# Gate matrix of an expert layer: float32 one-hot products replaced by three bfloat16 products per token

## The chip, the cores and the metric

The kernel runs on one core of a Trainium2 chip. The core has TensorE (PE, matrix products, with its weight loads shown apart as PEld), VectorE (DVE), ScalarE (ACT), GpSimd (POOL) and SyncE (SP, which here issues the DMAs). The metric is the device time of one execution in microseconds (us).

## What is computed

A two-layer encoder over 512 tokens of width 1024. Layer 0 mixes tokens by neighbourhood attention, layer 1 by a short gated convolution; behind each stands a PEER channel mixer over 128 x 128 = 16384 experts of one neuron each:

```
q = (xc @ w_query).reshape(c, 8, 2, 128)              # 8 heads, two halves
sc = einsum('chpd,hpnd->chpn', q, keys32)
sv, si = top_k(sc, 16)                                # per half
cand = sv[:, :, 0, :, None] + sv[:, :, 1, None, :]
best, pos = top_k(cand, 16)                           # 16 experts per head
eidx = take_along_axis(cidx, pos)                     # i * 128 + j
g = softmax(best)
a = einsum('cd,chkd->chk', xc, w_up[eidx])
act = gelu(a) * g
y = einsum('chk,chkd->cd', act, w_down[eidx])
```

So each token has 128 chosen experts (i, j) with a gate g each.

## The kernel before

**Two ways for the tokens.** Of the four chunks of 128 tokens, the last gets its experts' rows one by one (indirect DMAs, L475). The other three (384 tokens, `TD`) are computed densely: for every block `b` of 128 experts, `dense_up` multiplies all 384 tokens with the block's up weights and takes the gelu, and `dense_down` multiplies that with the gates and then with the down weights. For this each token needs its gates as a full matrix of 128 x 128, which is zero but for its 128 experts.

**The gate matrix.** That matrix is itself a product on PE: per token, a one-hot of the 128 chosen `i` (tile `ob`, from `iT`) and a one-hot of the 128 chosen `j`, scaled with the gates (tile `oa`, from `jT` and `gT`). `retrieval` goes over the 384 tokens in groups of four (96 groups per layer, 192 in all): DVE makes `ob` (L448) and `oa` (L452 for two of the tokens, scaled by ACT at L458; L460 for the two others), PE makes four products of 128 x 128 x 128 in float32 (L462, recorded as two passes each), ACT moves the result from PSUM to `stage` (L463). After 32 tokens `stage` is written to the buffer `gd` in DRAM (L466). The expert phase reads it back by blocks of experts, tile `gt` (L516); a read of `gt` takes from all twelve writes of the layer, so the first one comes after the last write.

**Products in two halves.** The dense products are float32 split in a high and a low part (`split`, L105 on ACT and L106 on DVE): three products with 384 columns for `ps_up` (L127), three with 512 columns for `acc` (L541). An up block has 24 products on PE.

**Order.** While DVE selects the experts and makes the one-hots, PE is given the up products of the first 52 blocks (`NPRE`); their results go to DRAM (`ad`). The generator `retrieval` tells the loop at L552 by its `yield` how much DVE and PE time its pieces take, and the loop puts up products between them. The order in the program is then set anew for each engine by the framework's scheduler as the kernel is built; on the chip each engine takes its instructions in that fixed order, and waits for semaphores. Up to six results of up blocks beyond the 52 are held on chip (`AHEAD`), so that a few more up blocks may be done before the expert phase begins. That phase's first step is `w`, the product of an up result with `gt` (L525), then its split `w_h`, `w_l`, then the first `acc`.

Of the kernel before, what the change touches and what calls it, by code (L numbers as in the profile page):

```python
# [12 lines left out]
F32 = mybir.dt.float32  # L13
F32R = mybir.dt.float32r
BF16 = mybir.dt.bfloat16
I32 = mybir.dt.int32
U32 = mybir.dt.uint32
AF = mybir.ActivationFunctionType
ALU = mybir.AluOpType
# [4 lines left out]
P = 128  # L24
# [16 lines left out]
NK = 128  # L41
# [8 lines left out]
TD = ND * P  # L50
NPRE = 52
PRE_RATE = 1.4
OB = 12
ACTN = 2
RING = 4
RAW = 3
LAST = 2
# [7 lines left out]
def encoder(ctx: ExitStack, tc: tile.TileContext, x, g_mix, g_ffn, g_ffn_row, g_fin_row, bias,  # L65
            w_qkv, w_o, w_in, w_conv, w_out, w_query, keys_t, up_t, up, down, out):
    nc = tc.nc
    const = ctx.enter_context(tc.tile_pool(name="const", bufs=1))
# [9 lines left out]
    iota = const.tile([P, P], F32, name="iota")  # L78
    nc.gpsimd.iota(iota, pattern=[[1, P]], base=0, channel_multiplier=0,
                   allow_small_or_imprecise_dtypes=True)  # L80
    thr = const.tile([P, TOPK], BF16, name="thr")
    ranks = const.tile([P, TOPK], BF16, name="ranks")
    for r in range(TOPK):
# [10 lines left out]
    def ps_acc(name):  # L94
        return ps_a.tile([P, 512], F32, name=name, tag="acc")
# [18 lines left out]
    def up_block(src, xh, xl, n):  # L114
        for ps in up_pieces(src, xh, xl, n):
            pass
        return ps
# [263 lines left out]
    def peer(l):  # L381
        xh, xl = norm_t(gf[:, l], f"f{l}")
        with ExitStack() as st:
            pp = st.enter_context(tc.tile_pool(name="peer", bufs=1))
            head = ExitStack()
            p2 = head.enter_context(tc.tile_pool(name="retrieval", bufs=2))
# [8 lines left out]
            for hp in range(2 * PH):  # L395
                kt = p2.tile([P, NK], F32, name="kt")
                nc.sync.dma_start(kt, keys_t[l, hp])
                ps = up_block(w_query[l, hp], xh, xl, S)
                qT = p2.tile([P, S], F32, name="qpT")
                nc.scalar.activation(qT, ps, AF.Copy)  # L400
                ps = ps_acc("ps_k")
                for c in range(NCH):
                    nc.tensor.matmul(ps[:, c * NK:(c + 1) * NK], qT[:, c * P:(c + 1) * P], kt, start=True, stop=True)  # L403
                hd, p = divmod(hp, 2)
# [4 lines left out]
            cand = p2.tile([P, PH, NCAND], F32, name="cand", bufs=1)  # L409
            nc.gpsimd.memset(cand, LOWEST)  # L410
            gT = p2.tile([P, TD], F32, name="gT", bufs=1)
            iT = p2.tile([P, TD], F32, name="iT", bufs=1)
            jT = p2.tile([P, TD], F32, name="jT", bufs=1)
            eid = pp.tile([P, P], F32, name="eid")
            eidx = pp.tile([P, P], I32, name="eidx")
            g3 = pp.tile([P, P], F32, name="g3")
# [1 line left out]
            pr = p2  # L418

            def retrieval():  # L420

                for c in (3, 0, 1, 2):
                    it = select(sv[:, c], si[:, c], pr, cand)
                    while True:
                        try:
                            yield next(it), 0.0
                        except StopIteration as e:
                            gg, ii, jj = e.value
                            break
                    if c == c3:  # L430
                        nc.vector.scalar_tensor_tensor(eid, ii, float(NK), jj, op0=ALU.mult, op1=ALU.add)
                        if l:
                            nc.vector.tensor_scalar(eid, eid, float(l * NK * NK), None, op0=ALU.add)
                        nc.vector.tensor_copy(eidx, eid)
                        nc.vector.tensor_copy(g3, gg)
                    else:
                        ps = ps_acc("ps_g")
                        for n, t in enumerate((gg, ii, jj)):
                            nc.tensor.transpose(ps[:, n * P:(n + 1) * P], t, ident)
                        for n, t in enumerate((gT, iT, jT)):  # L440
                            nc.vector.tensor_copy(t[:, c * P:(c + 1) * P], ps[:, n * P:(n + 1) * P])
                for t0 in range(0, TD, GT):
                    stage = pr.tile([P, NK, GT], F32, name="stage", tag="big")
                    for q in range(GT // 4):
                        ps = ps_acc("ps_gb")
                        t = t0 + 4 * q
                        b4 = pr.tile([P, 4, NK], F32, name="ob", bufs=OB // 4)
                        nc.vector.tensor_tensor(b4, iota[:, None, :].to_broadcast([P, 4, NK]),  # L448
                                                iT[:, t:t + 4, None].to_broadcast([P, 4, NK]), op=ALU.is_equal)
                        a4 = pr.tile([P, 4, NK], F32, name="oa", bufs=OB // 4)  # L450
                        if ACTN:
                            nc.vector.tensor_tensor(a4[:, :ACTN], iota[:, None, :].to_broadcast([P, ACTN, NK]),  # L452
                                                    jT[:, t:t + ACTN, None].to_broadcast([P, ACTN, NK]),
                                                    op=ALU.is_equal)
                        for n in range(4):
                            a, t = a4[:, n], t0 + 4 * q + n
                            if n < ACTN:
                                nc.scalar.activation(a, a, AF.Copy, scale=gT[:, t:t + 1])  # L458
                            else:
                                nc.vector.tensor_scalar(a, iota, jT[:, t:t + 1], gT[:, t:t + 1],  # L460
                                                        op0=ALU.is_equal, op1=ALU.mult)
                            nc.tensor.matmul(ps[:, n * NK:(n + 1) * NK], a, b4[:, n], start=True, stop=True)  # L462
                        nc.scalar.activation(stage[:, :, 4 * q:4 * q + 4].rearrange("p i t -> p t i"),  # L463
                                             ps.rearrange("p (t i) -> p t i", t=4), AF.Copy)
                        yield 1.35, 0.9
                    nc.sync.dma_start(gd[t0 // GT], stage)  # L466

# [84 lines left out]
            for d, p in retrieval():  # L552
                dve += d
                pe += p
                while pe < dve * PRE_RATE and next(pre, 0) is None:
                    pe += 0.49
# [3 lines left out]
            p2 = st.enter_context(tc.tile_pool(name="experts", bufs=2))  # L560
# [111 lines left out]
    for l in range(DEPTH):  # L672
        if l % 2 == 0:
            attention(l)
        else:
            short_conv(l)
        peer(l)
# [76 lines left out]
```

## Time and profile before

| | |
|---|---|
| median of 3 runs | 2993.33 us (2993.03 to 2993.86) |
| profiled execution, its own time | 2994.69 us |
| span of its instructions | 2992.9 us |
| PE busy | 2952.2 us (99%) |
| DVE busy | 2345.6 us (78%) |
| ACT busy | 1360.9 us (45%) |
| granted TensorE clock, mean | 0.996 |

The durations are those of the profiled execution; its time is 1.4 us above the median and 1.8 us above its span. Busy time of PE counts modelled ends, so products that follow each other overlap in the records: how fast they go is read from their starts.

### The profile page before, as it was taken

How to read it: one execution, taken by the hardware profiler on the slowest of the kernel's cores; microseconds unless marked ns; L12 is line 12 of the kernel's file. 1: busy time of each engine (PE TensorE's matmuls, PEld its weight loads, DVE VectorE, ACT ScalarE, POOL GpSimd, SP SyncE). 2: the span in 40 equal slices, each digit the busy share in tenths (PEclk: the TensorE clock that was granted, in tenths of full speed). 3: DMA queues.
4: the chain of work that ended last, by engine and by line, in shares of the span. 5: the costliest groups of instructions: out<-in, count | busy, mean ns of one | idle time of the engine just before them, and what ended most of it. 6: DMA issues, size and time to landing. Idle time of an engine off the chain costs nothing.

```text
span 2992.9 us, 43780 instructions
## 1 busy us (share of the span) xinstructions
PE 2952.2 (99%) x15570; PEld 2636.1 (88%) x15570; DVE 2345.6 (78%) x5115; ACT 1360.9 (45%) x2237; POOL 663.4 (22%) x571
## 2 busy tenths in 40 slices
PE   8999999999999999999999999999999999999998
PEld 6777899999888888888878789999988888888886
DVE  5445999886888888878864489998788888888786
ACT  5453257994333333333332323699733333333333
POOL 0000000002343444343400000000043434444341
PEclk9999999999999999999999999999999999999999
DMA  5323355659999999999933324556799999999995
GB/s 187 106 81 96 95 161 168 240 214 328 335 337 346 335 343 329 337 343 324 320 113 93 117 87 129 166 216 217 261 352 348 334 347 332 338 330 346 325 329 190
DMA packets 297979, 747.93 MB, mean 250 GB/s; under 512 B 23456, under 2 KB 139168, under 8 KB 294688
## 3 DMA queue, kind: packets, MB, share of 16 engines
q1 hardware_dynamic: 224032, 476.67, 46.5%
q0 software_dynamic: 73728, 268.47, 24.7%
q8 instruction: 122, 2.00, 0.3%
q14 instruction: 97, 0.79, 0.1%
HBM read 672.17 MB, written 72.88 MB: 249 GB/s over the span
## 4 chain that ended last, share of the span: by engine, by line
PE 91%; DVE 4%; issue 2%; DMA 2%; ACT 1%; POOL 0%; DVEq 0%; POOLq 0%; SPq 0%
PE ps_up L127 45%; PE acc L541 33%; PE ps_gb L462 6%; PE ps_o L191 3%; DVE wu_l L106 1%; PE ps_k L403 1%; PE ps_s L260 1%; PE ps_o L300 1%; DMA row<-in_up,eidx 1%; PE ps_pt L286 1%; DMA gd<-stage 0%; PE ps_t L175 0%; POOL row L475 0%; DVE tk L600 0%; ACT sq L150 0%
## 5 line engine op out<-in xcount | busy, mean ns | idle before, releaser
L127 PE MATMUL ps_up<-xhf,wu_l 128*128 128x384 f32 (+1 forms) x2304 | 798.4, 347 | 1.1 <-DVE wu_l L106 1.0
L127 PE MATMUL ps_up<-xhf,wu_h 128*128 128x384 f32 (+1 forms) x2304 | 794.3, 345 | 2.3 <-ACT ab L504 2.0
L127 PE MATMUL ps_up<-xlf,wu_h 128*128 128x384 f32 (+1 forms) x2304 | 792.4, 344 | 0.0
L105 ACT ACTIVATE wu_h<-wu_raw 128x1024 fp32r<-128x1024 f32 x336 | 355.4, 1058 | 688.8 <-PE ps_up L127 413.2
L475 POOL DMA_INDIRECT row<-in_up,eidx x256 | 325.1, 1270 | 1277.9 <-DMA wu_raw<-in_up_t 848.5
L541 PE MATMUL acc<-wd_h,w_l 128*128 128x512 f32 x1536 | 601.4, 392 | 0.1
L541 PE MATMUL acc<-wd_l,w_h 128*128 128x512 f32 x1536 | 601.2, 391 | 0.0
L105 ACT ACTIVATE wd_h<-wd_raw 128x1024 fp32r<-128x1024 f32 x256 | 271.5, 1061 | 699.2 <-issue 591.0
L106 DVE TENSOR_TENSOR wu_l<-wu_raw,wu_h 128x1024 fp32r<-128x1024 f32 x336 | 411.1, 1224 | 191.2 <-ACT wu_h L105 190.1
L541 PE MATMUL acc<-wd_h,w_h 128*128 128x512 f32 x1536 | 513.0, 391 | 0.9 <-ACT w_h L105 0.9
L106 DVE TENSOR_TENSOR wd_l<-wd_raw,wd_h 128x1024 fp32r<-128x1024 f32 x256 | 313.6, 1225 | 231.3 <-ACT wd_h L105 230.7
L127 PEld LDWEIGHTS ps_up<-xhf,wu_h 128*128 128x128 f32 x2304 | 433.3, 188 | 20.9 <-ACT ab L504 3.4
L127 PEld LDWEIGHTS ps_up<-xlf,wu_h 128*128 128x128 f32 x2304 | 433.1, 188 | 17.3
L127 PEld LDWEIGHTS ps_up<-xhf,wu_l 128*128 128x128 f32 x2304 | 433.1, 188 | 16.8 <-DVE wu_l L106 3.8
L475 POOL DMA_INDIRECT row<-in_down,eidx x256 | 332.4, 1298 | 510.4 <-DVE sq L482 471.8
L541 PEld LDWEIGHTS acc<-wd_h,w_l 128*128 128x128 f32 x1536 | 288.2, 188 | 59.5 <-DVE w_l L106 1.2
L491 DVE SCALAR_TENSOR_TENSOR accg<-row,ag,accg 128x1024 f32<-128x1024 f32 x256 | 327.9, 1281 | 15.8 <-DMA row<-in_down,eidx 15.1
L541 PEld LDWEIGHTS acc<-wd_l,w_h 128*128 128x128 f32 x1536 | 288.3, 188 | 59.0
L541 PEld LDWEIGHTS acc<-wd_h,w_h 128*128 128x128 f32 x1536 | 287.0, 188 | 55.3 <-ACT w_h L105 2.3
L482 DVE SCALAR_TENSOR_TENSOR sq<-row,hn 128x1024 bf16<-128x1024 f32 x256 | 312.5, 1221 | 6.2 <-DMA row<-in_up,eidx 5.0
L462 PE MATMUL ps_gb<-ob,oa 128*128 128x128 f32 x1536 | 209.4, 274 | 0.0
L463 ACT ACTIVATE stage<-ps_gb 128x512 f32<-128x512 f32 x192 | 204.5, 1114 | 2.0 <-PE ps_gb L462 1.4
(162 smaller groups left out, 3262.6 us busy)
## 6 DMA issues: line engine op xcount, KB each, us to landing
wd_raw<-in_down SPq DMA_DIRECT2D x256, 512.0 KB, 6.0
wu_raw<-in_up_t SPq DMA_DIRECT2D x256, 512.0 KB, 5.1
gd<-stage SPq DMA_DIRECT2D x24, 2048.0 KB, 7.2
gt<-gd SPq DMA_DIRECT2D x64, 768.0 KB, 9.6
ad<-ab SPq DMA_DIRECT2D x104, 192.0 KB, 2.4
at<-ad SPq DMA_DIRECT2D x52, 384.0 KB, 8.1
wu_raw<-in_w_query SPq DMA_DIRECT2D x32, 512.0 KB, 3.5
wu_raw<-in_w_qkv SPq DMA_DIRECT2D x24, 512.0 KB, 3.7
```

The costliest lines, as they stand in the source:

```text
L105: nc.scalar.activation(hi, raw, AF.Copy)
L106: nc.vector.tensor_tensor(lo, raw, hi.bitcast(F32), op=ALU.subtract)
L127: nc.tensor.matmul(ps[:, :n], a[:, c], b[:, kc, :n], start=k == 0, stop=k == 3 * KC - 1)
L191: nc.tensor.matmul(ps[c], a[:, m, c * P:(c + 1) * P], b, start=m == 0 and i == 0, stop=m == KC - 1 and i == 2)
L260: nc.tensor.matmul(ps[hh][:, a * 256:(a + 1) * 256], t["q"][hs, j * P:(j + 1) * P], kk[hs, :, BAND0[j]:BAND0[j] + BAND], start=True, stop= ...
L286: nc.tensor.transpose(pt[:, i * P:(i + 1) * P], sc[:, a, half * P:(half + 1) * P], ident)
L462: nc.tensor.matmul(ps[:, n * NK:(n + 1) * NK], a, b4[:, n], start=True, stop=True)
L463: nc.scalar.activation(stage[:, :, 4 * q:4 * q + 4].rearrange("p i t -> p t i"), ps.rearrange("p (t i) -> p t i", t=4), AF.Copy)
L475: nc.gpsimd.indirect_dma_start(out=t, out_offset=None, in_=table, in_offset=bass.IndirectOffsetOnAxis(ap=eidx[:, k:k + 1], axis=0))
L482: nc.vector.scalar_tensor_tensor(o, t, 1.0, hn, op0=ALU.mult, op1=ALU.mult, accum_out=ag[:, k:k + 1])
L491: nc.vector.scalar_tensor_tensor(accg, t, ag[:, k:k + 1], accg, op0=ALU.mult, op1=ALU.add)
L541: nc.tensor.matmul(acc[c, half], aa[:, cs], ww[:, hs], start=new and i == 0, stop=n == NK - 1 and ww is held[-1][-1])
```

## The change

The gates are split exactly into three bfloat16 parts (tile `gp`): the first is the gate rounded to bfloat16, the next the rounded rest, the third the rest of that. The indices go to bfloat16 (`ijT`, exact up to 127). Both one-hots of four tokens come from one DVE operation (`hot`, 2 x 128 x 4 elements, token innermost), and a second one multiplies the `j` half with the three parts (`cut`, 3 x 128 x 4). PE then makes three bfloat16 products per token into one PSUM sum, 12 per group, with operands that lie four elements apart. The eviction reads PSUM in another order and writes runs of four to `stage`. ACT no longer scales one-hots.

```diff
@@ -78,6 +77,8 @@
+    iota4 = const.tile([P, NK, 4], BF16, name="iota4")
+    nc.vector.tensor_copy(iota4, iota[:, :, None].to_broadcast([P, NK, 4]))
@@ -409,8 +410,8 @@
             gT = p2.tile([P, TD], F32, name="gT", bufs=1)
-            iT = p2.tile([P, TD], F32, name="iT", bufs=1)
-            jT = p2.tile([P, TD], F32, name="jT", bufs=1)
+            ijT = p2.tile([P, 2, TD], BF16, name="ijT", bufs=1)
+            gp = p2.tile([P, 3, TD], BF16, name="gp", bufs=1)
@@ -437,31 +438,32 @@
-                        for n, t in enumerate((gT, iT, jT)):
-                            nc.vector.tensor_copy(t[:, c * P:(c + 1) * P], ps[:, n * P:(n + 1) * P])
+                        cs = slice(c * P, (c + 1) * P)
+                        for n, t in enumerate((gT[:, cs], ijT[:, 0, cs], ijT[:, 1, cs])):
+                            nc.vector.tensor_copy(t, ps[:, n * P:(n + 1) * P])
+
+                        for n in range(3):
+                            nc.vector.tensor_copy(gp[:, n, cs], gT[:, cs])
+                            if n < 2:
+                                nc.vector.tensor_tensor(gT[:, cs], gT[:, cs], gp[:, n, cs], op=ALU.subtract)
...
-                        b4 = pr.tile([P, 4, NK], F32, name="ob", bufs=OB // 4)
-                        nc.vector.tensor_tensor(b4, iota[:, None, :].to_broadcast([P, 4, NK]),
-                                                iT[:, t:t + 4, None].to_broadcast([P, 4, NK]), op=ALU.is_equal)
-                        a4 = pr.tile([P, 4, NK], F32, name="oa", bufs=OB // 4)
-                        if ACTN:
-                            nc.vector.tensor_tensor(a4[:, :ACTN], iota[:, None, :].to_broadcast([P, ACTN, NK]),
-                                                    jT[:, t:t + ACTN, None].to_broadcast([P, ACTN, NK]),
-                                                    op=ALU.is_equal)
+                        hot = pr.tile([P, 2, NK, 4], BF16, name="hot", bufs=OB // 4)
+                        nc.vector.tensor_tensor(hot, iota4[:, None].to_broadcast([P, 2, NK, 4]),
+                                                ijT[:, :, None, t:t + 4].to_broadcast([P, 2, NK, 4]),
+                                                op=ALU.is_equal)
+                        cut = pr.tile([P, 3, NK, 4], BF16, name="cut", bufs=OB // 4)
+                        nc.vector.tensor_tensor(cut, hot[:, 1:2].to_broadcast([P, 3, NK, 4]),
+                                                gp[:, :, None, t:t + 4].to_broadcast([P, 3, NK, 4]), op=ALU.mult)
                         for n in range(4):
-                            a, t = a4[:, n], t0 + 4 * q + n
-                            if n < ACTN:
-                                nc.scalar.activation(a, a, AF.Copy, scale=gT[:, t:t + 1])
-                            else:
-                                nc.vector.tensor_scalar(a, iota, jT[:, t:t + 1], gT[:, t:t + 1],
-                                                        op0=ALU.is_equal, op1=ALU.mult)
-                            nc.tensor.matmul(ps[:, n * NK:(n + 1) * NK], a, b4[:, n], start=True, stop=True)
-                        nc.scalar.activation(stage[:, :, 4 * q:4 * q + 4].rearrange("p i t -> p t i"),
-                                             ps.rearrange("p (t i) -> p t i", t=4), AF.Copy)
+                            for i in range(3):
+                                nc.tensor.matmul(ps[:, n * NK:(n + 1) * NK], cut[:, i, :, n], hot[:, 0, :, n],
+                                                 start=i == 0, stop=i == 2)
+                        nc.scalar.activation(stage[:, :, 4 * q:4 * q + 4],
+                                             ps.rearrange("p (t i) -> p i t", t=4), AF.Copy)
                         yield 1.35, 0.9
```

The scheduler gives the instructions another order, though the `yield` values are the same. On PE, before, the last gate groups of layer 0 stand among single up products (`xhf`, `xlf` are the two halves of the activations, `wu_h`, `wu_l` those of the weights; a row `ps_gb` x4 is one group):

```order
L127 MATMUL ps_up<-xhf_2381,wu_h 128x384
L127 MATMUL ps_up<-xlf_2382,wu_h 128x384
L462 MATMUL ps_gb<-ob,oa 128x128 x4
L127 MATMUL ps_up<-xhf_2381,wu_l 128x384
L127 MATMUL ps_up<-xhf_2381,wu_h 128x384
L127 MATMUL ps_up<-xlf_2382,wu_h 128x384
L127 MATMUL ps_up<-xhf_2381,wu_l 128x384
L462 MATMUL ps_gb<-ob,oa 128x128 x4
L127 MATMUL ps_up<-xhf_2381,wu_h 128x384
L127 MATMUL ps_up<-xlf_2382,wu_h 128x384
```

The second of these two groups is the layer's last. From there 95 up products follow on PE, in both layers, up to the first products of the expert phase, which stand so:

```order
L127 MATMUL ps_up<-xhf_2381,wu_l 128x384
L127 MATMUL ps_up<-xhf_2381,wu_h 128x384
L127 MATMUL ps_up<-xlf_2382,wu_h 128x384
L541 MATMUL acc_7311<-wd_h,w_h 128x512
L541 MATMUL acc_7315<-wd_h,w_h 128x512
```

At the same place of PE, with the change, the last rows of layer 0's gate products and the first of the expert phase are (LDWEIGHTS is the load of one part of `cut`, which is an instruction of its own for bfloat16):

```order
L463 LDWEIGHTS cut
L463 MATMUL ps_gb<-hot,cut 128x128
L463 LDWEIGHTS cut
L463 MATMUL ps_gb<-hot,cut 128x128
L543 MATMUL acc_7712<-wd_h,w_h 128x512
L543 MATMUL acc_7716<-wd_h,w_h 128x512
```

No up product is left between the two in layer 0, and 9 are in layer 1. Within the stretch from the first gate product to the last, 840 and 831 up products stand in the two layers in place of 675, and 577 in place of 601 between the last key scores and the first gate product; most of the stretch now goes in turns of 36 gate products (three groups) and 25 up products.

On DVE, the one-hots of those three groups stand together, with one low half of an up block's weights (`wu_l`) in each turn:

```order
L107 TENSOR_TENSOR wu_l<-wu_raw,wu_h 128x1024
L455 TENSOR_TENSOR hot<-iota_82,ijT 128x1024 x2
L459 TENSOR_TENSOR cut<-hot,gp 128x1536
L455 TENSOR_TENSOR hot<-iota_82,ijT 128x1024
L459 TENSOR_TENSOR cut<-hot,gp 128x1536 x2
L107 TENSOR_TENSOR wu_l<-wu_raw,wu_h 128x1024
```

Before, a group had `ob`, one `oa` of 256 elements and two `oa` of 128 there, and the groups stood one by one.

## Rows read from the trace of the kernel before

**Rows 1.** The page: busy time by engine, and the granted clock in 40 slices.

```profile
PE 2952.2 (99%) x15570; PEld 2636.1 (88%) x15570; DVE 2345.6 (78%) x5115; ACT 1360.9 (45%) x2237; POOL 663.4 (22%) x571
...
PEclk9999999999999999999999999999999999999999
```

**Rows 2.** Windows: us, busy of PE, PEld, DVE, ACT, POOL, clock; last `ps_gb` alone.

```profile
450.00:486.00 36.00, 35.00 (x202) 34.33 (x201) 35.22 (x131) 23.05 (x29) 0.00 (x0) 1.00 0.49 156
500.00:650.00 150.00, 150.00 (x1069) 150.00 (x1069) 133.37 (x316) 139.31 (x258) 0.00 (x0) 1.00 0.63 227
...
500.00:650.00 150.00, 78.15 (x575) 76.60 (x576) 75.68 (x71) 1.00 0.63 227
```

**Rows 3.** Timeline of PE, dense products: start us, length, instruction.

```profile
698.27 0.33 PE L127 MATMUL ps_up<-xhf,wu_h 128*128 128x384 f32 x1
...
706.24 0.34 PE L127 MATMUL ps_up<-xlf,wu_h 128*128 128x384 f32 x1
...
712.08 0.39 PE L541 MATMUL acc<-wd_h,w_h 128*128 128x512 f32 x1
...
715.48 0.39 PE L541 MATMUL acc<-wd_h,w_h 128*128 128x512 f32 x1
```

**Rows 4.** Groups of gate instructions: count, busy us, mean ns, idle before.

```profile
L462 PE MATMUL ps_gb<-ob,oa 128*128 128x128 f32 x1536 | 209.4, 274 | 0.0
...
L463 ACT ACTIVATE stage<-ps_gb 128x512 f32<-128x512 f32 x192 | 204.5, 1114 | 2.0 <-PE ps_gb L462 1.4
L448 DVE TENSOR_TENSOR ob<-iota,iT 128x512 f32<-128x512 f32 x192 | 132.1, 690 | 23.8 <-PE ps_gb L462 21.3
L458 ACT ACTIVATE oa<-oa,gT 128x128 f32<-128x128 f32 x384 | 130.5, 390 | 28.0 <-DVE oa L452 27.9
L460 DVE TENSOR_SCALAR oa<-iota,jT,gT 128x128 f32<-128x128 f32 x384 | 115.7, 345 | 0.0
...
L452 DVE TENSOR_TENSOR oa<-iota,jT 128x256 f32<-128x256 f32 x192 | 80.9, 421 | 0.0
```

**Rows 5.** Timeline of PE around one gate group.

```profile
599.77 1.05 PE L462 MATMUL ps_gb<-ob,oa 128*128 128x128 f32 x8
600.58 0.42 PE L127 MATMUL ps_up<-xhf,wu_l 128*128 128x384 f32 x1
600.84 0.34 PE L127 MATMUL ps_up<-xhf,wu_h 128*128 128x384 f32 x1
```

**Rows 6.** Timeline of the hand-off in layer 0, all engines.

```profile
689.05 1.05 PE L462 MATMUL ps_gb<-ob,oa 128*128 128x128 f32 x8
...
690.14 1.11 ACT L463 ACTIVATE stage<-ps_gb 128x512 f32<-128x512 f32 x1
691.27 0.33 SPq L466 DMA_DIRECT2D gd<-stage  x1
...
698.65 1.76 SPq L516 DMA_DIRECT2D gt<-gd  x2
...
705.57 0.56 DVE L525 TENSOR_TENSOR w<-ab,gt 128x384 f32<-128x384 f32 x1 [5.48 <-DMA gt<-gd]
...
706.79 1.63 PE L541 MATMUL acc<-wd_h,w_h 128*128 128x512 f32 x6 [0.21 <-ACT w_h L105]
```

**Rows 7.** PE's timeline ahead of layer 1's experts; two windows, clock and GB/s.

```profile
1718.69 0.66 PE L175 MATMUL ps_t<-ident,hs 128*128 128x128 f32 x2 [5.39 <-issue]
...
1717.00:1724.00 7.00, 5.31 (x25) 5.23 (x26) 4.99 (x28) 3.55 (x10) 0.00 (x0) 0.52 0.27 75
691.00:698.00 7.00, 7.00 (x42) 7.00 (x42) 1.23 (x1) 1.92 (x4) 0.00 (x0) 1.00 0.96 378
```

**Rows 8.** Groups of DVE instructions that resemble the new ones.

```profile
L106 DVE TENSOR_TENSOR wu_l<-wu_raw,wu_h 128x1024 fp32r<-128x1024 f32 x336 | 411.1, 1224 | 191.2 <-ACT wu_h L105 190.1
...
L643 DVE TENSOR_TENSOR msk<-msk,ds 128x2048 bf16<-128x2048 bf16 x16 | 19.8, 1240 | 0.0
...
L648 DVE TENSOR_TENSOR msk<-msk 128x1024 bf16<-128x1024 bf16 x16 | 11.3, 706 | 0.0
```

More of the change, by code (lines that the diff above doesn't have):

```diff
@@ L53 @@
 OB = 12
-ACTN = 2
 RING = 4
```

## The prediction

> **What bounds the kernel now.** I read the busy shares first. TensorE (PE) is busy through the whole span and its clock is full in every slice [rows 1]; the other engines have room. Then the stretch that the change touches, the gate products, by windows: from 500 to 650 us PE is busy 150.0 of 150.0 us, ScalarE (ACT) 139.3, VectorE (DVE) 133.4 [rows 2]. A busy PE may hide short waits, since its ends are modelled, so I checked the start-to-start steps in the timeline. Dense products of 384 columns start from 698.27 to 706.24 us in 46 steps, 173.3 ns each; those of 512 columns from 712.08 to 715.48 in 15 steps, 226.7 ns each [rows 3]. The difference is 53.4 ns for 128 columns, and above its columns each product costs 173.3 - 160.2 = 13 ns. PE keeps these steps through the stretch, so its own work sets the pace there, and what it saves there is saved in the end, unless a wait appears.
>
> Last I looked at the way out of the stretch in the timeline: the last `stage` goes to DRAM and comes back as `gt` before the expert phase can begin [rows 6].
>
> **The gate products.** They are 192 groups of 4 tokens, 8 passes each [rows 4]. One group stands at 599.77 us, the next product at 600.58, and the one after that 0.26 us later in place of 0.173 [rows 5]: 0.81 + 0.087 = 0.897 us per group, 112 ns per pass. That is two times 53.4 ns plus 5 ns: a float32 pass streams its 128 columns at half rate. 192 x 0.897 = 172.2 us.
>
> After, a group is 12 pairs of weight load and product with 128 bfloat16 columns. No row shows one. If the columns stream at full rate and the load hides, a pair costs 53.4 ns plus what a product costs above its columns: 5 ns by the short passes of now, 13 by the long dense ones, so 59 or 67 ns. I take 63, as the pair is short like the first and streams at full rate like the second. 12 x 63 = 0.756 us, 145.2 in all: **-27.0 us** (-36.3 at 59, -17.8 at 67).
>
> **The hand-off to the expert phase.** In the order of before, 95 up products stand on PE between the last gate product and the first `acc`; in the order of the change none in the first layer, 9 in the second. What lies between takes its time on other queues [rows 6]: the last gate group starts at 689.05 us and frees PE at 689.95; `stage` is evicted from 690.14, its write to `gd` is issued at 691.27, the read `gt` at 698.65 when the write has landed, `w` starts at 705.57, and after it and its high half the first `acc` at 706.79. That is 16.8 us, and the 95 products (95 x 0.173 = 16.5) cover all but some 0.4 us of it. The second layer's hand-off has the same instructions and 95 products too, so I take it as equal. The up products that stood there are not gone, they stand earlier, where PE was full already; PE's total stays and the chain becomes idle time: 16.8 + (16.8 - 9 x 0.173) - 2 x 0.4 = **+31 us**. The bounds: with fewer weight loads beside it, the write can be shorter. From 691 to 698 us the queues moved 378 GB/s, the 2 MB of `gd` being only part [rows 7]; 2.1 MB at that rate take 5.5 us in place of 7.3, and as much may be gained on `gt`: 13 us per layer, +23.5. A slower eviction adds a microsecond per layer, +33.
>
> **The clock after the gap.** After PE stood idle for 5.4 us up to 1718.7, the granted clock was 0.52 over 1717 to 1724, near its lower level of 1.2 GHz [rows 7]. A gap of 15 us should do it too. Half speed for 3.4 to 7 us costs 1.7 to 3.5 us per layer; I take **+3.4 us** for both, 0 and +7 as ends.
>
> **DVE's way to the first gate product.** Per chunk of tokens the change adds three casts and two subtractions of 128x128. The nearest row, an `oa` of that size, takes 345 ns [rows 4], so they take up to 1.7 us per chunk and 5.2 per layer of three chunks. From 450 to 486 us DVE is busy 35.2 of 36.0 us, and PE, 35.0 busy, already waits 1.0 us [rows 2]; with the change 577 up products cover PE there in place of 601, 24 x 0.173 = 4.2 us less. The cost is nothing if the order keeps PE fed, and 9 us per layer if nothing does. I take 3, since most of the casts stand between other work of DVE after the first gate product has its operands: **+6 us**.
>
> **What costs nothing.** The one-hots on DVE: now 690 + 421 + 2 x 345 = 1801 ns per group [rows 4]. `hot` has 1024 elements in bfloat16 and `cut` 1536; bfloat16 two-input operations take 706 ns for 1024 and 1240 for 2048, also with an operand that repeats [rows 8], so 706 + 971 = 1677 ns. DVE has no more to do than now, and PE's stream covers it. ACT loses two scalings of 390 ns per group [rows 4]; nobody waited for them for long, so this gains nothing. The eviction reads PSUM with a hop for each element and writes runs of 4, where it now reads a run and writes with hops (1114 ns); I take the same 1.1 us, which ACT's freed time covers. The `iota4` copy at the start lies beside the first loads.
>
> **Sum.** -27.0 + 31 + 3.4 + 6 = +13.4 us on the profiled execution's own 2994.7, so 3008.1; the median of the runs is 1.4 lower: **3007 us**, 0.4% slower. 0.2%, 6 us, is about what a measurement of this kernel can tell from no change. With these terms the change pays only if a pair p takes less than 57 ns (192 x (0.897 - 12p) = 40.4). The case's own range is 2997 to 3025: the pair's ends, and up to half of what hand-off, clock and DVE's way may add.
>
> **The rivals.**
> *The hand-off shrinks (faster).* If it takes 13 us per layer, DVE's way to the first product costs 2 us in all, and pairs take 59 ns: -36.3 + 23.5 + 3.4 + 2 = -7.4, so **2986**. With that hand-off it isn't faster once a pair takes 62 ns or more. For it: the queues moved more than the write alone. Against: both transfers have a landing time that fewer neighbours don't remove, and 13 us is the end of my bounds.
> *No change.* Pairs at 59 ns with all else as in the sum: +4, so **2997**.
> *The weight load doesn't hide.* A 128-column bfloat16 product gives the load of the next 128 columns only 53 ns, where the passes of now give it 107 [rows 5]. If it shows in part, a pair lies between 67 and the 112 of now; the middle, 90, gives 1.08 us per group, +35 + 40 = +75, so **3069** (3120 at 112). For it: no product here is that short. Against: the passes of now show only 5 ns above their columns. The Trainium skill ("TensorE: Matmul & The Clock Gate", section "Back-to-back issue gap") puts a steady stream of load and product at 128 columns at about 81 ns; no run here shows that yet, and it would give 972 ns per group and some 3047 us.
> *DVE runs the new operands at one element per cycle*, as the float32 split does (1024 in 1224 ns [rows 8]): 1224 + 1760 per group is 1.2 us more than now, 115 us per layer where DVE has 23 to spare: about **3190**. Against it: `msk` repeats an operand and keeps the fast rate.
> *The eviction becomes the limit.* ACT has 139.3 us for 71 groups [rows 2], 1.96 each; without the scalings 1.18, the eviction's 1.11 among them. PE's group then takes 2.11 - 0.897 + 0.756 = 1.97, so ACT binds once the eviction takes 1.9 us. At 2.0 us some 20 us come on top: **3027**.
>
> **How the numbers follow.** The sum 0.40, no change 0.20, faster 0.15, the weight load 0.15, DVE 0.05, eviction 0.05. So faster 0.15, same 0.20, slower 0.65. Below 2984 and above 3060 lies about 0.2: the far end of the faster case, the upper half of the weight loads, and DVE.
>
> **What would show it.** Right: steps of 59 to 67 ns from one gate product to the next; PE idle once per layer, 13 to 17 us, right behind the last gate group, released by `w_h`, with a lower granted clock behind it; `hot` near 700 and `cut` near 970 ns; ACT's share in the stretch down by a third. Wrong: no idle time there, since the order would then not be what sets it; steps over 80 ns; PE waiting for `cut` all through the stretch.

## The result, and the profile after

| | before | changed |
|---|---|---|
| median of 4 runs each | 2993.3 us (2993.0 to 2993.9) | 3133.5 us (3131.9 to 3135.6) |
| profiled execution, its own time | 2994.7 us | 3135.6 us |
| ratio | | 1.0468, 95% interval 1.0455 to 1.0481 |

The changed kernel is slower by 140 us, where 14 were forecast; the case's own range ended at 3025 us, 32 above the kernel before, and 3060 us was the upper mark of the chances. The page of the changed kernel, busy time by engine:

```profile
PE 3062.8 (98%) x16338; PEld 2729.3 (87%) x16338; DVE 2360.5 (75%) x4762; ACT 1179.8 (38%) x1853; POOL 659.3 (21%) x571
```

TensorE is still the busy engine, and its mean granted clock is 0.990 (0.996 before): a difference of 0.006 is at most some 19 us of the 3134, so no loss of clock explains 140. The groups of the gate stage, over the whole span (count, busy us, mean ns, idle before), which answer to [rows 4]:

```profile
L463 PE MATMUL ps_gb<-hot,cut 128*128 128x128 bf16 x2304 | 286.6, 297 | 0.0
L459 DVE TENSOR_TENSOR cut<-hot,gp 128x1536 bf16<-128x1536 bf16 x192 | 178.0, 953 | 0.1
L455 DVE TENSOR_TENSOR hot<-iota,ijT 128x1024 bf16<-128x1024 bf16 x192 | 132.2, 690 | 138.1 <-PE ps_gb L463 137.7
L465 ACT ACTIVATE stage<-ps_gb 128x512 f32<-128x512 f32 x192 | 115.0, 599 | 253.0 <-PE ps_gb L463 253.0
L446 DVE CAST gp<-gT 128x128 bf16<-128x128 f32 x18 | 4.0, 224 | 0.0
L448 DVE TENSOR_TENSOR gT<-gT,gp 128x128 f32<-128x128 f32 x12 | 3.4, 286 | 0.0
```

VectorE's two operations take 690 and 953 ns, and `hot` now waits 137.7 us in all for `ps_gb`: VectorE stands behind TensorE, not the other way round. ScalarE waits for it too, and its eviction takes 599 ns in place of 1114. TensorE's timeline around one turn of three gate groups, to be held against [rows 5]:

```profile
605.20 4.41 PE L463 MATMUL ps_gb<-hot,cut 128*128 128x128 bf16 x36
609.35 0.42 PE L128 MATMUL ps_up<-xlf,wu_h 128*128 128x384 f32 x1
609.62 0.34 PE L128 MATMUL ps_up<-xhf,wu_l 128*128 128x384 f32 x1
```

The mean length of a record, 297 ns, says little, since the records overlap. The starts do: from 605.20 to 609.35 there are 36 products, and the first up product behind them takes 0.27 us to the next start in place of 0.173. That makes (4.15 + 0.097) / 36 = **118 ns per pair** of load and product, 1.415 us per group. Before, a group took 0.897. 192 x 0.518 is 99 us.

The hand-off in layer 0, all engines, to be held against [rows 6]:

```profile
767.90 1.58 PE L463 MATMUL ps_gb<-hot,cut 128*128 128x128 bf16 x12
...
770.14 0.33 SPq L468 DMA_DIRECT2D gd<-stage  x1
...
777.40 1.16 SPq L518 DMA_DIRECT2D gt<-gd  x2
...
782.72 0.56 DVE L527 TENSOR_TENSOR w<-ab,gt 128x384 f32<-128x384 f32 x1 [12.48 <-DMA gt<-gd]
783.36 0.52 ACT L106 ACTIVATE w_h<-w 128x384 fp32r<-128x384 f32 x1 [13.25 <-DVE w L527]
...
783.94 1.65 PE L543 MATMUL acc<-wd_h,w_h 128*128 128x512 f32 x3 [14.46 <-ACT w_h L106]
...
2307.15 2.93 PE L543 MATMUL acc<-wd_h,w_h 128*128 128x512 f32 x6 [12.75 <-ACT w_h L106]
```

The chain of before stands there without its cover: TensorE is idle for 14.5 us, released by `w_h`, and for 12.8 us in layer 1 (last row). Windows of the changed kernel (us, busy of PE, PEld, DVE, ACT, POOL, granted clock, DMA share, GB/s):

```profile
500.00:650.00 150.00, 150.00 (x1060) 145.71 (x1059) 102.54 (x132) 55.98 (x88) 0.00 (x0) 1.00 0.47 176
784.00:787.50 3.50, 3.50 (x9) 2.92 (x10) 2.73 (x5) 1.17 (x3) 0.00 (x0) 0.50 1.05 389
787.50:791.00 3.50, 3.50 (x15) 3.41 (x14) 1.89 (x4) 0.00 (x0) 1.19 (x2) 0.68 1.03 408
450.00:486.00 36.00, 32.36 (x183) 30.94 (x182) 34.96 (x130) 20.74 (x24) 0.00 (x0) 1.00 0.42 141
```

Behind the gap the clock stands at 0.50, which is 1.2 GHz, and then at 0.68: 3.5 x 0.5 + 3.5 x 0.32 = 2.9 us are lost in this layer; in layer 1 it is 0.50 from 2307 to 2311 us, another 2. Ahead of the gate stage TensorE is busy for 32.4 of 36 us in layer 0, where it was 35.0 [rows 2], and for 32.8 in layer 1 (1975 to 2011 us; 35.0 in the same stretch before): 2.6 and 2.2 us more of idle time. In layer 1 the clock also falls to 0.57 there from 1998 to 2002 us, another 1.7 us. So 99 (products) + 27.3 - 0.8 (hand-off) + 5 + 1.7 (clock) + 4.8 (ahead of the first gate product) = 137 of the 140.9 us between the profiled executions; 4 are not assigned. Open was why a pair takes 118 ns.

### The profile page after: what moved, and what is told of

It reads as the page before. It is cut to its first block, busy times and chain, and to the rows that moved or that the text cites. A ratio compares the mean times of both kernels' runs of the same rounds, so it can differ in the third digit from the quotient of the medians.

```text
span 3133.8 us, 44260 instructions
## 1 busy us (share of the span) xinstructions
PE 3062.8 (98%) x16338; PEld 2729.3 (87%) x16338; DVE 2360.5 (75%) x4762; ACT 1179.8 (38%) x1853; POOL 659.3 (21%) x571
## 4 chain that ended last, share of the span: by engine, by line
PE 46%; DVE 3%; DMA 1%; issue 0%; ACT 0%; DVEq 0%; ACTq 0%; SPq 0%
PE ps_up L128 22%; PE acc L543 17%; PE ps_gb L463 4%; PE ps_o L192 1%; DVE wu_l L107 1%; PE ps_k L404 0%; PE ps_t L176 0%; DMA row<-in_down,eidx 0%; DMA gd<-stage 0%; DVE tk L602 0%; DMA gt<-gd 0%; DVE pos L601 0%; DVE h L595 0%; DVE pos L604 0%; ACT sq L151 0%
## 5 line engine op out<-in xcount | busy, mean ns | idle before, releaser
L107 DVE TENSOR_TENSOR wd_l<-wd_raw,wd_h 128x1024 fp32r<-128x1024 f32 x256 | 313.4, 1224 | 217.2 <-ACT wd_h L106 207.7
L463 PE MATMUL ps_gb<-hot,cut 128*128 128x128 bf16 x2304 | 286.6, 297 | 0.0
L463 PEld LDWEIGHTS <-cut 128*128 128x128 bf16 x2304 | 258.4, 117 | 16.4 <-issue 11.2
```

The costliest lines, as they stand in the source:

```text
L107: nc.vector.tensor_tensor(lo, raw, hi.bitcast(F32), op=ALU.subtract)
L463: nc.tensor.matmul(ps[:, n * NK:(n + 1) * NK], cut[:, i, :, n], hot[:, 0, :, n], start=i == 0, stop=i == 2)
```

## The experiments

All are edits of the changed kernel, but for the last. The ratios are to the kernel before, run beside each on the same chip; pair times are read from starts as above.

**Which operand?** Three runs read one operand or both as 128 neighbouring elements of the same tiles (2 bytes apart) instead of every fourth (8 bytes apart).

```diff
 # weights packed
-nc.tensor.matmul(ps[:, n * NK:(n + 1) * NK], cut[:, i, :, n], hot[:, 0, :, n],
+nc.tensor.matmul(ps[:, n * NK:(n + 1) * NK], cut[:, i].rearrange("p k n -> p (k n)")[:, n * NK:(n + 1) * NK], hot[:, 0, :, n],
 # moving operand packed
+nc.tensor.matmul(ps[:, n * NK:(n + 1) * NK], cut[:, i, :, n], hot[:, 0].rearrange("p k n -> p (k n)")[:, n * NK:(n + 1) * NK],
```

Both packed. 

> Same instructions, but both operands of the 2304 gate products are read as 128 neighbouring elements of the same tiles instead of 128 elements that lie 8 bytes apart (so the products multiply the wrong elements; everything else is computed as in the changed kernel). In the changed kernel a load and its product follow each other in 118 ns; 2304 pairs, so each ns of a pair is 2.3 us of the span. Theory A, the spacing of the elements costs the time: the pair falls to about 63 ns (the float32 gate product of before took 224 ns for four such passes, 56 each), and the time to 3133.5 - 2304 x 0.055 = 3007 us (3000 to 3030; VectorE, 1.64 us a group, may then be waited for). Theory B, a bfloat16 load and product of 128 columns take 118 ns however the operands lie: 3133 us (3128 to 3139).

Weights alone. 

> Only the weights of the gate products are read as 128 neighbouring elements, the moving operand stays 8 bytes apart (the products multiply the wrong elements). Theory A1, it is the load of spaced weights that takes 118 ns: pair about 63 ns, 3007 us (3000 to 3030). Theory A2, it is the spaced moving operand that slows the product: pair stays at 118 ns, 3133 us. Theory B, neither: 3133 us.

Moving operand alone. 

> Only the moving operand of the gate products is read as 128 neighbouring elements, the weights stay 8 bytes apart (the products multiply the wrong elements). Theory A1, the load of spaced weights takes 118 ns: 3133 us. Theory A2, the spaced moving operand slows the product: pair about 63 ns, 3007 us (3000 to 3030). Theory B: 3133 us. If both spacings cost something, the two single changes share the gain of the double one.

| packed | median us | ratio to before, 95% interval |
|---|---|---|
| both | 2995.4 | 1.0007, 0.9997 to 1.0016 |
| weights | 3129.0 | 1.0454, 1.0437 to 1.0472 |
| moving operand | 2996.9 | 1.0011, 1.0001 to 1.0021 |

TensorE's timeline with the weights packed, one turn:

```profile
612.18 4.34 PE L463 MATMUL ps_gb<-hot,cut 128*128 128x128 bf16 x36
616.27 0.43 PE L128 MATMUL ps_up<-xhf,wu_l 128*128 128x384 f32 x1
616.53 0.34 PE L128 MATMUL ps_up<-xhf,wu_h 128*128 128x384 f32 x1
```

And with the moving operand packed:

```profile
609.74 2.20 PE L463 MATMUL ps_gb<-hot,cut 128*128 128x128 bf16 x36
611.75 0.42 PE L128 MATMUL ps_up<-xhf,wu_h 128*128 128x384 f32 x1
612.01 0.33 PE L128 MATMUL ps_up<-xlf,wu_h 128*128 128x384 f32 x1
```

(4.09 + 0.09) / 36 = 116 ns against (2.01 + 0.09) / 36 = 58, and 56 from one gate product to the next inside a burst. The moving operand alone makes the pair slow. The weights, still 8 bytes apart in the second timeline, cost nothing: the load hides even behind a product of 56 ns. Theory A2 holds; A1 and B are out.

**How far apart?** Two runs read the moving operand 4 and 16 bytes apart, a third the weights 16 bytes apart.

```diff
+hot.rearrange("p c k n -> p (c k n)")[:, 256 * n:256 * (n + 1):2]       # moving, 4 bytes
+hot.rearrange("p c k n -> p (c k n)")[:, n::8]                          # moving, 16 bytes
+cut.rearrange("p i k n -> p (i k n)")[:, n + 128 * i:n + 128 * i + 1024:8]   # weights, 16 bytes; moving packed
```

4 bytes. 

> The changed kernel with the moving operand of the gate products read 4 bytes apart (every second element) instead of 8 (so the products multiply the wrong elements). Theory P, a product streams at half rate as soon as its elements are not neighbours: pair 118 ns, 3129 to 3134 us. Theory Q, what counts is the bytes that a product passes over: at half the spacing the pair falls to 56 ns or somewhere between (87 ns: 3062 us), 2997 us if it is free.

16 bytes. 

> The same with the moving operand read 16 bytes apart (every eighth element; wrong elements again). Theory P, half rate at any spacing: pair 118 ns, 3129 to 3134 us. Theory Q, bytes passed over: twice the spacing, twice the time, about 236 ns a pair, 3133.5 + 2304 x 0.118 = 3405 us.

Weights, 16 bytes. 

> The changed kernel with the moving operand of the gate products packed and the weights read 16 bytes apart (wrong elements in both). Theory W, the weight load reads at the same bytes per time as the moving operand but beside it: at 16 bytes a load takes some 230 ns, no longer hides behind a 56 ns product, and the time is 2997 + 2304 x (0.230 - 0.056) = 3398 us. Theory V, spacing costs the load nothing: pair 56 ns, 2997 us, as with weights 8 bytes apart.

They took 3005.8, 3467.4 and 3008.9 us, in one execution each. TensorE's timeline of one turn at 4 bytes:

```profile
605.04 2.31 PE L463 MATMUL ps_gb<-hot,cut 128*128 128x128 bf16 x36
607.16 0.42 PE L128 MATMUL ps_up<-xhf,wu_l 128*128 128x384 f32 x1
```

At 16 bytes, and the window of that stage:

```profile
611.97 8.46 PE L463 MATMUL ps_gb<-hot,cut 128*128 128x128 bf16 x36
620.07 0.68 PE L128 MATMUL ps_up<-xhf,wu_l 128*128 128x384 f32 x1
620.55 0.52 PE L128 MATMUL ps_up<-xhf,wu_h 128*128 128x384 f32 x1
620.87 0.52 PE L128 MATMUL ps_up<-xlf,wu_h 128*128 128x384 f32 x1
```

```profile
500.00:650.00 150.00, 150.00 (x674) 106.89 (x672) 65.80 (x86) 36.28 (x56) 0.00 (x0) 0.77 0.31 118
```

Two windows inside that one burst, the gate products and their eviction alone (us, busy of PE and ACT, granted clock, DMA share, GB/s):

```profile
612.00:615.50 3.50, 3.50 (x16) 0.56 (x1) 1.00 0.29 116
616.00:619.50 3.50, 3.50 (x17) 0.60 (x1) 0.50 0.02 5
```

Weights at 16 bytes:

```profile
606.45 2.44 PE L463 MATMUL ps_gb<-hot,cut 128*128 128x128 bf16 x36
608.70 0.42 PE L128 MATMUL ps_up<-xhf,wu_l 128*128 128x384 f32 x1
```

A pair takes 56, 61, 118 and 225 to 230 ns with the moving elements 2, 4, 8 and 16 bytes apart. From 4 bytes on the time goes with the bytes that the product passes over: 128 x 4 bytes in 61 ns, 128 x 8 in 118, 128 x 16 in 230, 8 to 9 bytes per ns and partition. Theory P is out, Q holds for these spacings. At 16 bytes the run is 62 us above Q's 3405: there the granted clock fell to 0.77 in the stage although TensorE had products all the time (128 columns in 230 ns each). It goes to and fro between its two levels, and the gate products keep their pace, with 16 and 17 of them in 3.5 us at 1.00 and at 0.50. The up products behind the burst lose by it: their starts are 0.48 and then 0.32 us apart instead of 0.173, and over both gate stages the steps from one up product to the next come to 84 us more than in the changed kernel. The weights are another matter: 16 bytes apart they cost 5 to 9 ns a pair (61 in the median, (2.25 + 0.09) / 36 = 65 in this turn; the whole run is 12 us longer than with weights 8 bytes apart), and theory W, 230 ns, is out.

**The hand-off.** The up products of the first dense block are queued on TensorE behind the last gate product (`gates[0]` is the last gate product's instruction).

```diff
-                    for _ in ups(nup, top):
-                        pass
+                    with tc.issue_after(gates[0]) if n == 0 else nullcontext():
+                        for _ in ups(nup, top):
+                            pass
```

> The changed kernel with the up products of the first dense block queued on TensorE behind the last gate product: 96 and 98 of them then stand between it and the first acc product, where 0 and 9 stood. If the bare hand-off costs what the trace shows (TensorE idle 14.8 us in layer 0 and 13.1 us in layer 1, then some 4 to 5 us at the granted clock that fell in the gap), the time falls by 27 to 33 us, to 3101 to 3107 us. Rival: the 96 products taken out of the gate stage had been cover there, and the gate stage gets as many idle microseconds as the hand-off loses: within 5 us of 3133.

3111.7 us, ratio 1.0395 (1.0378 to 1.0413): 22 us back, not 27 to 33. TensorE's end of the gate stage in that run:

```profile
705.79 3.01 PE L465 MATMUL ps_gb<-hot,cut 128*128 128x128 bf16 x24
710.45 5.85 PE L465 MATMUL ps_gb<-hot,cut 128*128 128x128 bf16 x48 [1.65 <-DVE cut L461]
716.55 4.48 PE L465 MATMUL ps_gb<-hot,cut 128*128 128x128 bf16 x36 [0.24 <-DVE cut L461]
...
739.54 0.42 PE L128 MATMUL ps_up<-xhf,wu_h 128*128 128x384 f32 x1
```

The idle time at the hand-off is gone in both layers. But the last gate groups now stand without up products between them, and there VectorE (0.690 + 0.953 us a group) is slower than TensorE (1.415): one wait of 1.65 us and one of 0.24 in each turn, 2.9 us of idle time a layer by the profile and 4.2 by the starts. Part of the rival was right: the products were cover, for a smaller sum.

**Versions that compute the same.** First, ScalarE copies the row one-hot into a packed tile, which the products stream:

```diff
+                        pk = pr.tile([P, 4, NK], BF16, name="pk", bufs=OB // 4)
+                        nc.scalar.activation(pk, hot[:, 0].rearrange("p k n -> p n k"), AF.Copy)
-                                nc.tensor.matmul(ps[:, n * NK:(n + 1) * NK], cut[:, i, :, n], hot[:, 0, :, n],
+                                nc.tensor.matmul(ps[:, n * NK:(n + 1) * NK], cut[:, i, :, n], pk[:, n],
```

> The changed kernel, computing the same, but ScalarE copies the row one-hot into a packed tile (4 x 128 neighbouring elements) and the products stream that one. If the spaced moving operand is the whole cost, a pair takes 56 ns as it did with the packed (wrong) operand, and the time starts from that run's 2997 us. The framework's order has 46 up products behind the last gate product here, where the changed kernel has 0 and 9: at 173 ns each they shorten the bare hand-off by some 7 us a layer, and with some clock back the time is 2980 us (2972 to 2990). Rival: the copy (512 elements, between the 599 ns that ScalarE's eviction of 512 takes and twice that) stands in front of each group and ScalarE is late with it: 3000 to 3030 us.

2989.7 us, ratio 0.9985 (0.9976 to 0.9994). The pair takes 56 ns and the copy 686. The time lies at the slow end of what was expected: with 46 up products (8 us) behind the last gate product TensorE is still idle for 9.3 and 8.9 us there, only 5.1 and 3.9 less than in the changed kernel.

```profile
710.18 1.22 PE L545 MATMUL acc<-wd_h,w_h 128*128 128x512 f32 x2 [9.33 <-ACT w_h L106]
```

The chain takes longer beside them: from the start of the last gate product of layer 0 to the first `acc` 17.6 us, where the changed kernel takes 14.8.

Then TensorE's order is forced as well, with the edit of the hand-off and this one:

```diff
-                while pe < dve * PRE_RATE and next(pre, 0) is None:
+                while pe < dve * PRE_RATE:
+                    with tc.issue_after(gates[0]) if gates else nullcontext():
+                        if next(pre, 0) is not None:
+                            break
                     pe += 0.49
```

> As the run with the packed copy, and TensorE's order is forced: the up products that the planner hands out after a gate group are queued behind that group, so that each of the 96 groups is followed by 6 of them, and 104 stand behind the last gate product. The bare hand-off goes (14.7 and 13.1 us, and the clock behind it). VectorE then sets the gate stage: 0.690 + 0.953 us a group and 0.3 for its share of the up blocks' split, 1.95 us, 187 us a layer, against 1.71 us of TensorE. Sum against the run with the spaced weights and packed moving operand (2997 us): hand-off and clock -36, idle of TensorE behind VectorE +23: 2984 us (2972 to 2996). Rival: VectorE keeps pace better than its busy time says and only the hand-off counts: 2961 us. Rival: the forced order makes TensorE wait for one-hots that used to be ahead, and all is lost: 3000 us and more.

2982.7 us, ratio 0.9964 (0.9953 to 0.9976), the fastest version here. Its windows, the gate stage and the hand-off of layer 0:

```profile
500.00:650.00 150.00, 149.55 (x1478) 136.12 (x1477) 147.72 (x198) 119.04 (x204) 0.00 (x0) 1.00 0.63 241
667.00:686.00 19.00, 19.00 (x116) 18.91 (x114) 6.02 (x7) 7.64 (x11) 4.66 (x4) 1.00 0.94 341
```

The hand-off of layer 0 is covered at full clock (4.0 us stay open in layer 1), and VectorE is now busy for 147.7 of 150 us. But TensorE is busy for 149.6 of them. Its timeline of one group:

```profile
600.50 0.86 PE L467 MATMUL ps_gb<-pk,cut 128*128 128x128 bf16 x12
601.18 0.42 PE L128 MATMUL ps_up<-xhf,wu_h 128*128 128x384 f32 x1
601.43 0.33 PE L128 MATMUL ps_up<-xlf,wu_h 128*128 128x384 f32 x1
...
602.32 0.86 PE L467 MATMUL ps_gb<-pk,cut 128*128 128x128 bf16 x12
```

The 12 gate products and the 6 up products behind them take 1.82 us without a wait, and in the whole run TensorE's gate products wait for `cut` once, 0.5 us. So TensorE itself sets this stage (182 us a layer, 0.6 us of them idle), and not VectorE as expected. That the forecast of 2984 was met is luck: the 23 us of waits for VectorE did not come. What took their place is the number of bursts, 190 in place of 81 in the run that it started from: each costs TensorE some 0.09 us more, most of it at the first up product behind it, whose next start comes after 0.25 us in place of 0.173. That is 10 us, and 4 more stay open at the hand-off.

Two runs took VectorE for the bound and tried to relieve it; by these rows they had next to nothing to win. In one, GpSimd makes the third part of `cut`:

```diff
+                        nc.gpsimd.tensor_tensor(cut[:, 2], hot[:, 1],
+                                                gp[:, 2, None, t:t + 4].to_broadcast([P, NK, 4]), op=ALU.mult)
```

> As the run with the packed copy and the forced order, computing the same, but GpSimd multiplies the third gate part (512 elements a group) and VectorE only the first two. In that run VectorE is busy for 147.7 of 150 us (500 to 650) and ScalarE 119; GpSimd does nothing there. If VectorE is the bound of that stage, its group falls from 0.690 + 0.953 to about 0.690 + 0.690 us, TensorE sets the stage (1.71 us a group instead of 1.9), and the time falls by some 8 us a layer: 2967 us (2960 to 2975). Rival: GpSimd takes over 1.9 us for its 512 products or slows VectorE's own reads, and the stage gets longer: 2990 us and more.

3079.6 us, ratio 1.0285 (1.0271 to 1.0299): the rival. Its groups, from 500 to 650 us:

```profile
L465 POOL TENSOR_TENSOR cut<-hot,gp 128x512 bf16<-128x512 bf16 x63 | 92.3, 1473 | 58.4 <-DVE hot L457 52.7 <-DVE gp L448 2.7 <-PE ps_gb L469 2.3
L457 DVE TENSOR_TENSOR hot<-iota,ijT 128x1024 bf16<-128x1024 bf16 x63 | 63.6, 1023 | 4.4 <-POOL cut L465 1.9
...
L463 DVE TENSOR_TENSOR cut<-hot,gp 128x1024 bf16<-128x1024 bf16 x63 | 56.2, 893 | 0.0
...
L107 DVE TENSOR_TENSOR wu_l<-wu_raw,wu_h 128x1024 fp32r<-128x1024 f32 x16 | 28.7, 1792 | 0.0
```

GpSimd's own 1473 ns would have fitted into a group. But `hot` goes from about 700 to 1023 ns, the split from 1224 [rows 8] to 1792, and `cut` with a third less work still takes 893. VectorE is slower while GpSimd computes beside it: in this same run the 62 `hot` that no GpSimd product overlaps take 678 ns in the mean, the 130 others 1144. (The Trainium skill, "GPSIMD Engine Reference", section "1. Specifications", says that the two share their SBUF interfaces; the trace agrees, with 1144 ns against 678.)

In the other, one VectorE operation makes the one-hots of eight tokens, so that `hot` lies 16 bytes apart:

```diff
+                        if q % 2 == 0:
+                            both = pr.tile([P, 2, NK, 8], BF16, name="hot", bufs=2)
+                            nc.vector.tensor_tensor(both, iota4[:, None].to_broadcast([P, 2, NK, 8]),
+                                                    ijT[:, :, None, t:t + 8].to_broadcast([P, 2, NK, 8]),
+                                                    op=ALU.is_equal)
+                        hot = both[:, :, :, q % 2 * 4:q % 2 * 4 + 4]
+                        pk = pr.tile([P, 4, NK], BF16, name="pk", bufs=2)
```

> As the run with the packed copy and the forced order, computing the same, but one VectorE operation makes the one-hots of eight tokens (2048 elements, every second group) in place of two with 1024 each. From 0.690 us for 1024 and 0.953 for 1536 elements an operation has a fixed part of 0.164 us, so VectorE saves 0.082 us of 1.95 a group, 7.9 us a layer. If VectorE sets that stage (147.7 of 150 us busy), the time falls by up to 16 us, less what TensorE's order gives back: 2971 us (2964 to 2978). Rival: the multiply that now reads pieces of four elements 16 bytes apart, or the copy that reads elements 16 bytes apart, gets slower and eats the gain: 2980 us and more.

2994.2 us, ratio 1.0005 (0.9996 to 1.0014): the rival again. Groups from 500 to 650 us:

```profile
L464 ACT ACTIVATE pk<-hot 128x512 bf16<-128x512 bf16 x81 | 106.9, 1321 | 1.4 <-DVE hot L459 1.4
...
L472 ACT ACTIVATE stage<-ps_gb 128x512 f32<-128x512 f32 x80 | 60.6, 760 | 0.0
...
L459 DVE TENSOR_TENSOR hot<-iota,ijT 128x2048 bf16<-128x2048 bf16 x40 | 49.2, 1229 | 7.3 <-ACT pk L464 7.3
```

```profile
500.00:650.00 150.00, 147.39 (x1439) 133.23 (x1439) 142.50 (x154) 148.64 (x201) 0.00 (x0) 1.00 0.62 236
```

VectorE gained as worked out (1229 ns for eight tokens), but the copy that reads 16 bytes apart takes 1321 ns where it took 679 at 8 bytes, and ScalarE, busy for 148.6 of 150 us, becomes the bound: VectorE waits for it. Its eviction goes from 598 to 760 ns as well, which no run explains. The edit also leaves `hot` (now of eight tokens) and `pk` two buffers in place of three; what that adds was not tried by itself.

**The eviction alone**, in the kernel before:

```diff
-                        nc.scalar.activation(stage[:, :, 4 * q:4 * q + 4].rearrange("p i t -> p t i"),
-                                             ps.rearrange("p (t i) -> p t i", t=4), AF.Copy)
+                        nc.scalar.activation(stage[:, :, 4 * q:4 * q + 4],
+                                             ps.rearrange("p (t i) -> p i t", t=4), AF.Copy)
```

> The kernel before with only the eviction turned: ScalarE writes the stage tile in the changed kernel's order (four neighbouring elements, read 512 bytes apart) instead of reading in order and writing 128 bytes apart; the same values. In the changed kernel that took the eviction from 1114 to 599 ns. If ScalarE was no bound of the gate stage before (TensorE busy throughout it), the time stays within 6 us of 2993 us, with ScalarE's busy time down by about 0.5 us a group. Rival: ScalarE, 139 of 150 us busy, did set the pace there with VectorE: 20 us and more faster.

2994.1 us, ratio 1.0001 (0.9992 to 1.0010). ScalarE's eviction, over the whole span, and the window of [rows 2]:

```profile
L463 ACT ACTIVATE stage<-ps_gb 128x512 f32<-128x512 f32 x192 | 112.2, 586 | 27.8 <-PE ps_gb L462 26.8
```

```profile
500.00:650.00 150.00, 150.00 (x1068) 150.00 (x1067) 133.40 (x316) 112.98 (x257) 0.00 (x0) 1.00 0.62 226
```

The eviction takes half the time and nothing is gained: ScalarE was no bound before, as expected.

## Why the prediction was wrong

**The products, the step that failed.** The prediction took -27.0 us from pairs of 63 ns, on two conditions: the columns stream at full rate, and the load hides. It weighed only the second, as the rival with pairs of up to 112 ns. The load hides (56 ns with a packed moving operand and weights 8 bytes apart). The first condition failed: the change reads `hot[:, 0, :, n]` 8 bytes apart, and at that spacing 128 columns take 118 ns. So the term is +99 us in place of -27. The text on the change said that the operands lie four elements apart, and no bound was set on it; every row the pair was worked out from streams packed operands. The rival of the weight load came nearest in time (3069, 3120 at its end) by another mechanism, one that the runs exclude. With 118 ns for 63 the sum gives 99.5 + 40.4 = 140 us, as measured: this one term accounts for the miss. That it fits to the microsecond is luck, since small errors of the other terms (below) cancel.

The Trainium skill ("Advanced Engine Details and Errata", section "SBUF Cachelines") would have made the spacing free: it asks for at least two hits on a line of 16 bytes, which elements 8 bytes apart give. The runs differ, with half the rate at 8 bytes, and they decide. The 81 ns that the prediction weighed, from the Trainium skill ("TensorE: Matmul & The Clock Gate", section "Back-to-back issue gap"), appear in no run: pairs take 56 ns or go by the spacing.

**The hand-off, right.** +31 forecast; TensorE's idle times of 14.5 and 12.8 us less what was open before make +27, inside the bounds. Covering it gave 22 us back of these and the clock's 5; most of the rest went to waits for VectorE.

**The clock, right.** +3.4 forecast with +7 as its end, some 5 read behind the gaps.

**The way to the first gate product, right.** +6 forecast, some 5 read; the casts take 224, the subtractions 286 ns, under the 345 assumed. But the first gate product of layer 0 starts at 486.46 us, at 486.36 before: VectorE's way got no longer, and TensorE idles more with 24 up products fewer there. Whether the casts add to that no run separates.

**VectorE, right.** 706 and 971 ns forecast, 690 and 953 measured; `hot` waits for TensorE. The rival of one element per cycle is out.

**The eviction, mis-sized without effect.** 1.1 us assumed, 0.60 measured; the run with the eviction alone shows that it is worth nothing to the time.

**The check of the sum.** Put 56 ns for 63 and the products give 192 x (0.897 - 0.672) = -43 us, so the sum is 2991 us. The runs with a packed moving operand took 2995.4 and 2996.9. The rest of the sum holds to within 0.2%, and so does the break-even that it gave, a pair of 57 ns.

## What to carry to other kernels

Count the bytes that a moving operand passes over, not its columns: on this chip a bfloat16 product of 128 columns took 56 ns packed, 61 at a spacing of 4 bytes and 118 at 8, while its weights could lie 16 bytes apart for 5 to 9 ns more. A layout that makes the producing engine fast (here the token innermost) is paid for by each reader, so look at what every reader does with it, and let an engine with room turn it for the one that sets the pace: ScalarE's copy brought 3133.5 us down to 2989.7, and with TensorE's order mended the change is worth 0.4% against the kernel before (2982.7 us). And when a scheduler gives a new order, look for what used to stand over a round trip through DRAM: 95 products had covered 17 us here.

## What was not expected of the hardware

- The moving operand's spacing sets its rate, some 9 bytes per ns and partition (118 ns at 8 bytes, 225 to 230 at 16), and at 16 bytes it is the same at either level of the clock; weights cost nothing 8 bytes apart and 5 to 9 ns a pair at 16.
- ScalarE's copy also doubles from 8 to 16 bytes: 679 and 1321 ns for 512 elements. Its eviction of 512 elements reads PSUM 512 bytes apart in 599 ns, while reading in order and writing 128 bytes apart took 1114 [rows 4].
- The granted clock fell to 0.77 in a stage where TensorE was never idle by the profile, but each gate product took 230 ns for 128 columns; with products of 118 ns the stage stayed at 1.00.
- GpSimd's products slowed VectorE's `hot` and split by nearly a half (the split from 1224 to 1792 ns), which cost far more than the work they took over.
